# The memory branch: loads issued from ScalarE, norms moved behind the queries, two gate products pulled ahead

## The chip, the core and the metric

The kernel is written for one core of a Trainium2 chip. Such a core has TensorE (matrix products, PE in the rows, with PEld for its weight loads), VectorE (DVE), ScalarE (ACT), GpSimd (POOL) and SyncE (SP), which only issues transfers here. Each engine works through its own instructions in the order in which the program was built; semaphores hold an instruction until what it needs is there. The metric is the device time of one execution in microseconds.

## The reference

Two blocks of two layers each run on 512 tokens of width 1024 in float32. The first block (dilated attention, a recurrence, two feed-forward layers) ends at about 1550 us of the trace and is not touched. The second block repeats this layer twice:

```
h = rmsnorm(x, norm_g);  z = h @ w_in            # w_in: 1024 x 7968
o_a, o_b = two attention branches of parts of z
mem_kv = rmsnorm(mem, mem_norm_g) @ w_mem_kv     # mem: 256 rows of 1024
o_m = softmax(norm(q) @ norm(k).T / sqrt(128)) @ v, 4 heads of 128   # q of z; k, v of mem_kv
g = sigmoid(merge part of z), three gates of 1024
x = x + (g0 * (o_a @ w_branch_a) + g1 * (o_b @ w_branch_b) + g2 * (o_m @ w_branch_m)) @ w_out
```

The change is in the branch of `mem`, which comes first in each of the two layers.

## The kernel before

Every float32 product is made of three products of a high and a low part (`mm3`, L43 to L47). A weight unit of 512 KB is loaded by `wunit` (L212, a load that SyncE issues into one of two `ws` buffers), and split: ScalarE writes the high part `wh` (a CAST at L204), VectorE the low part `wl` (a subtraction at L204). There are four `wh` and four `wl` buffers, which come free when TensorE has read them. Of TensorE's eight output banks three are called `acc`, two `tr`, two `sc`, one `pv`.

The end of the layer before already computes the queries of the memory branch (`second_first`): one `acc` bank for each group of 128 tokens, groups 0 to 2 ahead of the branch, and group 3 when the branch asks for it. Each bank takes 24 products of 128x512, and the four weight units of the queries fill all four `wh` buffers until group 3 is through.

`memory` then copies each bank into two `zc` tiles (ScalarE, L1397; three buffers), and norms each: square (L813, ScalarE), sum and scaling (L815, L816, VectorE), a power (L817, GpSimd), two multiplications (L818, L1399, VectorE). It is turned by TensorE (L856, into a `tr` bank, two transposes for a tile) and split again (L204). The 256 rows of `mem` are loaded as two tiles, normed by `normed` (L309 ScalarE, L300 VectorE, L302 GpSimd, L312 VectorE), and turned by `turned` (L320, 16 transposes into `acc` and `sc` banks). Then come the products for keys and values (rows `acc<-wh,st`), which read the turned rows.

`weave` (L945 on) runs a branch step by step and, after the steps that a table PLANS names, one step of a filler. The filler is `branch`: gate products of 24 matmuls in two steps, and output products of 12 in one. A step is 12 matmuls whichever it is. What the branches leave of the filler runs on its own at the layer's end. A scheduler that simulates the program at build time sets the final order on each engine; `behind` keeps it from placing an instruction ahead of another that is named.

In a transfer or product, the rows name what is written, `<-`, and what is read; in a product the moving operand stands first.

Of the kernel before, what the change touches and what calls it, by code (L numbers as in the profile page):

```python
# [18 lines left out]
D = 1024  # L19
NT = T // 128  # L20
KD = D // 128
# [8 lines left out]
LRU_BUFS = 24  # L30
NORMALIZE_AFTER, VALUES_AFTER = 5, 6
LRU_STEPS = (0, 1, 2, range(4), "v", 3, range(4, 8), "vvv")
PLANS = ((16,),
         (8, 13, 13, 14, 15, 18, 19, 19, 22, 22, 25, 26, 26, 27, 27, 28, 28, 29, 29, 35, 35, 37, 38, 39),
         (1, 5, 5, 8, 8, 10, 12, 15, 16, 17, 19, 21, 32, 32, 34, 35, 38))
TURN_BANKS = (("acc", "sc"), ("acc", "sc"), ("sc", "tr"), ("tr", "pv"))
# [132 lines left out]
class Net:  # L169
# [618 lines left out]
    def state(self, shape, dt=F32R):  # L788
        return self.lt("st", shape, dt)

    def small_bc(self, row, n, name):
        t = self.lt(name, [128, n])
        self.nc.sync.dma_start(t, row[None, :].to_broadcast([128, n]))
        return t

    def rope_tables(self, g, scale=1.0):
# [160 lines left out]
    def second_layer(self, l, z2):  # L957
        nc, i, tc = self.nc, self.i, self.tc
        w_in, h = i["w_in_2"][l], self.h
        with tc.tile_pool(name=f"sec{l}", bufs=1) as self.lp:  # L960
            lp = self.lp
            u, o_m, o_a, o_b = [], [], [], []
            br = [self.branch(l, h, o, i[f"w_branch_{x}_2"][l], b, u) for o, x, b in ((o_m, "m", 2), (o_a, "a", 0), (o_b, "b", 1))]
            self.weave(self.memory(l, h, w_in, z2, o_m), br[0], PLANS[0])
            self.weave(self.nsa(l, h, w_in, o_a), itertools.chain(br[0], br[1]), PLANS[1])
            self.weave(br[0])
            self.weave(self.fox(l, h, w_in, o_b), itertools.chain(br[1], br[2]), PLANS[2])
# [40 lines left out]
    def branch(self, l, h, o, w, b, u):  # L1008
# [9 lines left out]
        def gate(m):  # L1018
            c = OFF_MG + b * D + m * 128
            wh, wl = self.wunit(wg[:, :, c:c + 128])  # L1020
            pg = self.bank()
            for k in range(KD):
                mm3(nc, pg, wh[:, k], wl[:, k], h[0][:, k], h[1][:, k], k == 0, k == KD - 1)
                if k == KD // 2 - 1:
                    yield
            t = self.lt("mt", [128, T])
            nc.scalar.activation(t, pg, AF.Tanh, scale=0.5)
            ts.append(t)
            yield
# [344 lines left out]
            nc.sync.dma_start(K[o:o + 2, e::2], self.cd[1, :, 4 * hf + e:4 * hf + 4:2])  # L1374


    def memory(self, l, h, w_in, z2, os):
        nc, i, lp = self.nc, self.i, self.lp
        lh, ll = self.rows(h)
        gq = self.small_bc(i["mem_q_norm_2"][l], 128, "gq")  # L1380
        gk = self.small_bc(i["mem_k_norm_2"][l], 128, "gk0")
        gm = self.lt("pt", [128, D])
        nc.sync.dma_start(gm, i["mem_norm_g_2"][l][None, :].to_broadcast([128, D]))
        mH, mL = self.state([128, KD, 256]), self.state([128, KD, 256])
        rows = []
        for t in range(2):
            mt, xn = self.lt("pt", [128, D]), self.lt("o", [128, D])
            nc.sync.dma_start(mt, i["mem_2"][0, t * 128:(t + 1) * 128])
            rows.append(self.normed(mt, gm, (xn[:, :512], xn[:, 512:], xn)))
        Q = [self.state([128, 2, 2, T]) for _ in range(2)]  # L1390
        for t, ps in enumerate(z2):
            if t >= 2:
                self.turned(rows[t - 2], (mH, mL), t - 2)
            cs = slice(t * 128, (t + 1) * 128)
            for c in range(2):
                zc = self.lt("zc", [128, 256])
                nc.scalar.copy(zc, ps[:, c * 256:c * 256 + 256])  # L1397
                qn = self.head_norm(zc, 2, 128)
                nc.vector.scalar_tensor_tensor(qn, qn, 128 ** -0.5, gq[:, None, :].to_broadcast([128, 2, 128]), op0=OP.mult, op1=OP.mult)  # L1399
                pt = self.transposed([qn[:, a] for a in range(2)])  # L1400
                self.split(Q[c][:, 0, :, cs], Q[c][:, 1, :, cs], pt[:, :256].rearrange("p (h q) -> p h q", h=2))
            yield
        wkv = i["w_mem_kv_2"][l]
        mlh, mll = self.rows((mH, mL))
        K = self.state([128, 2, 4, 256])
# [136 lines left out]
```

## Time and profile before

| | us |
|---|---|
| median of 3 runs | 2842.91 (2842.14 to 2843.55) |
| the profiled execution | 2847.33 |
| its span, first to last instruction | 2845.2 |
| TensorE busy | 2752.4 |
| VectorE busy | 1655.0 |
| ScalarE busy | 1285.5 |
| GpSimd busy | 509.2 |
| mean granted clock of TensorE | 0.988 |

TensorE is busy nearly throughout, so time is lost where it idles or where its granted clock is below 1. The memory branch begins at about 1550 us in layer 0 and at about 2205 us in layer 1, and the rows below are of these two places.

### The profile page before, as it was taken

Reading aid. Unit: us, or ns where it says so; the run is one execution under the profiler, and the core shown is the slowest. Engines: PE = TensorE matmul, PEld = TensorE weight load, DVE = VectorE, ACT = ScalarE, POOL = GpSimd, SP = SyncE. Lnnn points to the kernel's source line nnn. Section 1 sums busy time; section 2 is a strip of 40 time slices with the busy share of each in tenths; the row PEclk is TensorE's granted clock in tenths of the full one; section 3 lists DMA queues with packets and bytes.
Section 4 is the critical chain, followed back from the end, with each engine's and each line's share of the span. In section 5 each row is a group of like instructions: output and inputs, shape, how many; then the busy total and the mean of one; then the engine's idle time right before and its main releaser. Section 6 shows DMA issues by size and latency. Waiting matters only on the chain.

```text
span 2845.2 us, 39405 instructions
## 1 busy us (share of the span) xinstructions
PE 2752.4 (97%) x14493; PEld 2338.7 (82%) x14493; DVE 1655.0 (58%) x3306; ACT 1285.5 (45%) x2518; POOL 509.2 (18%) x682
## 2 busy tenths in 40 slices
PE   7999999799999998999998999999999899999999
PEld 6788888688888887888887898789878798788987
DVE  3245555555542678555425687776744677777753
ACT  3234344344432465444323554666533554665542
POOL 0001101111100000111001242333320242333420
PEclk9999999899999999999999999999999999999999
DMA  5553443333332343433323424122234423113233
GB/s 172 171 169 86 104 94 86 118 111 97 97 126 96 112 122 108 126 96 97 126 97 114 125 74 109 38 54 75 71 93 141 137 70 109 34 46 84 71 93 107
DMA packets 386071, 288.52 MB, mean 101 GB/s; under 512 B 33576, under 2 KB 339496, under 8 KB 385880
## 3 DMA queue, kind: packets, MB, share of 16 engines
q1 hardware_dynamic: 376752, 268.94, 32.9%
q10 hardware_dynamic: 9128, 17.07, 1.6%
q8 instruction: 115, 1.88, 0.3%
q14 instruction: 76, 0.62, 0.1%
HBM read 266.86 MB, written 21.20 MB: 101 GB/s over the span
## 4 chain that ended last, share of the span: by engine, by line
PE 82%; DVE 8%; DMA 4%; ACT 3%; issue 2%; POOL 1%; SPq 0%; ACTq 0%; DVEq 0%; POOLq 0%
PE acc L45 20%; PE acc L46 20%; PE acc L47 20%; PE tr L856 2%; PE sc L45 2%; PE sc L46 2%; PE sc L47 2%; DVE wl L204 2%; PE pv L916 2%; PE tr L45 2%; PE tr L47 1%; PE tr L46 1%; PE pv L46 1%; PE pv L47 1%; DMA ws<-in_attn_w_qkv_dram 1%
## 5 line engine op out<-in xcount | busy, mean ns | idle before, releaser
L204 DVE TENSOR_TENSOR wl<-ws,wh 128x1024 fp32r<-128x1024 f32 (+2 forms) x476 | 563.9, 1186 | 686.8 <-ACT wh L204 680.8
L204 ACT CAST wh<-ws 128x1024 fp32r<-128x1024 f32 (+2 forms) x476 | 469.5, 987 | 819.7 <-PE acc L46 303.6
L45 PE MATMUL acc<-hH,wh 128*128 128x512 f32 (+1 forms) x1928 | 742.3, 386 | 12.2 <-ACT gate L769 6.2
L46 PE MATMUL acc<-hL,wh 128*128 128x512 f32 (+1 forms) x1928 | 741.3, 385 | 1.5 <-DVE hL L204 1.2
L47 PE MATMUL acc<-hH,wl 128*128 128x512 f32 (+1 forms) x1928 | 739.5, 384 | 1.0 <-DVE wl L204 1.0
L45 PEld LDWEIGHTS acc<-hH,wh 128*128 128x128 f32 x1928 | 363.3, 189 | 83.6 <-ACT gate L769 6.6
L47 PEld LDWEIGHTS acc<-hH,wl 128*128 128x128 f32 x1928 | 363.9, 189 | 69.2 <-DVE wl L204 1.5
L46 PEld LDWEIGHTS acc<-hL,wh 128*128 128x128 f32 x1928 | 364.1, 189 | 68.4 <-DVE hL L204 2.5
L45 PE MATMUL acc<-wh,hH 128*128 128x256 f32 (+3 forms) x864 | 267.3, 312 | 5.4 <-ACT hH L204 4.1
L46 PE MATMUL acc<-wl,hH 128*128 128x256 f32 (+3 forms) x864 | 266.9, 310 | 2.3 <-DVE wl L204 2.3
L47 PE MATMUL acc<-wh,hL 128*128 128x256 f32 (+3 forms) x864 | 264.9, 309 | 0.1
L45 PEld LDWEIGHTS acc<-wh,hH 128*128 128x128 f32 x864 | 165.6, 192 | 14.5 <-ACT hH L204 4.5
L46 PEld LDWEIGHTS acc<-wl,hH 128*128 128x128 f32 x864 | 165.7, 192 | 11.9 <-DVE wl L204 3.7
L47 PEld LDWEIGHTS acc<-wh,hL 128*128 128x128 f32 x864 | 165.3, 191 | 7.4 <-DVE hL L204 0.4
L645 POOL TENSOR_TENSOR cv<-cv 128x512 f32<-128x512 f32 x48 | 62.0, 1292 | 465.1 <-DVE cv L582 448.4
L582 DVE SCALAR_TENSOR_TENSOR cv<-acc,cw,cv 128x511 f32<-128x511 f32 (+1 forms) x192 | 142.5, 746 | 3.2
L856 PE MATMUL tr<-ident,P 128*128 128x128 f32 x720 | 123.3, 277 | 10.7 <-DVE pt L204 5.2
L817 POOL TENSOR_TENSOR hst<-hst,mhalf 128x4 f32<-128x4 f32 (+2 forms) x90 | 91.0, 1017 | 223.5 <-DVE hst L816 221.7
L889 ACT ACTIVATE P<-P,soft 128x128 f32<-128x128 f32 (+1 forms) x192 | 108.1, 563 | 49.9 <-DVE soft L888 45.7
L888 DVE CUSTOM_DVE_ANT_0 P<-sc,causal 128x128 f32<-128x128 f32 (+1 forms) x192 | 92.9, 486 | 45.8 <-PE tr L856 31.5
L891 POOL TENSOR_SCALAR P<-P,soft,ngate 128x128 f32<-128x128 f32 (+3 forms) x128 | 83.9, 658 | 153.6 <-DVE soft L890 117.5
L204 DVE TENSOR_TENSOR pt<-tr,pt 128x128 fp32r<-128x128 f32 (+2 forms) x224 | 104.1, 474 | 11.8 <-ACT pt L204 10.4
(452 smaller groups left out, 4770.1 us busy)
## 6 DMA issues: line engine op xcount, KB each, us to landing
ws<-in_w_in_dram SPq DMA_DIRECT2D x116, 512.0 KB
ws<-in_ffn_w_up_dram SPq DMA_DIRECT2D x96, 512.0 KB
ws<-in_attn_w_qkv_dram SPq DMA_DIRECT2D x72, 512.0 KB
ws<-in_ffn_w_down_dram SPq DMA_DIRECT2D x48, 512.0 KB
x<-x ACTq DMA_DIRECT2D x16, 512.0 KB
ws<-in_lru_w_in_dram SPq DMA_DIRECT2D x16, 512.0 KB
ws<-in_w_mem_kv_dram SPq DMA_DIRECT2D x16, 512.0 KB
ws<-in_w_out_dram SPq DMA_DIRECT2D x16, 512.0 KB
```

The costliest lines, as they stand in the source:

```text
L45: nc.tensor.matmul(out, lh, rh, start=start, stop=False)
L46: nc.tensor.matmul(out, lh, rl, start=False, stop=False)
L47: return nc.tensor.matmul(out, ll, rh, start=False, stop=stop)
L204: return nc.scalar.copy(hi, src), (eng or nc.vector).tensor_tensor(lo, src, hi.bitcast(F32), op=OP.subtract)
L582: nc.vector.scalar_tensor_tensor(dst[:, s:], ps[:, :T - s], cw(taps - 1 - s), dst[:, s:], op0=OP.mult, op1=OP.add)
L645: nc.gpsimd.tensor_tensor(g, g, v, op=OP.mult)
L817: nc.gpsimd.tensor_tensor(st[:, 1], st[:, 0], self.mhalf[:rows, :nh], op=OP.pow)
L856: self.nc.tensor.transpose(ps[:, a * 128:(a + 1) * 128], s, self.ident)
L888: nc.vector.tensor_tensor_reduce(out=P, in0=S, in1=self.causal[:, 512 - n:512], scale=-1.0, scalar=BIG, op0=OP.add, op1=OP.min, accum_out=m)
L889: nc.scalar.activation(P, P, AF.Exp, bias=m, scale=-1.0, accum_out=s)
L891: nc.gpsimd.tensor_scalar(P, P, r, mult, op0=OP.mult, op1=OP.mult)
L916: nc.tensor.matmul(ps[:, lo:256], v(j), p[:, j, lo:], start=first and j == 0 and u == 0, stop=last and j == nj - 1 and u == 1)
```

## The change

Five loads (two gain vectors, the two tiles of `mem`, the gain of the memory norm) are issued by ScalarE instead of SyncE, the tiles ahead of their gain. `normed` of both tiles stands behind the last query tile's split, `turned` of both behind the second of two gate products. These two gates are the first four steps of the filler, which `memory` takes itself after the queries; the one step that the table took later is gone.

```diff
-PLANS = ((16,),
+PLANS = ((),
...
-    def small_bc(self, row, n, name):
+    def small_bc(self, row, n, name, eng=None):
         t = self.lt(name, [128, n])
-        self.nc.sync.dma_start(t, row[None, :].to_broadcast([128, n]))
+        (eng or self.nc.sync).dma_start(t, row[None, :].to_broadcast([128, n]))
...
-                mm3(nc, pg, wh[:, k], wl[:, k], h[0][:, k], h[1][:, k], k == 0, k == KD - 1)
+                self.last_gate = mm3(nc, pg, wh[:, k], wl[:, k], h[0][:, k], h[1][:, k], k == 0, k == KD - 1)
...
-        gq = self.small_bc(i["mem_q_norm_2"][l], 128, "gq")
-        gk = self.small_bc(i["mem_k_norm_2"][l], 128, "gk0")
+        gq = self.small_bc(i["mem_q_norm_2"][l], 128, "gq", nc.scalar)
+        gk = self.small_bc(i["mem_k_norm_2"][l], 128, "gk0", nc.scalar)
         gm = self.lt("pt", [128, D])
-        nc.sync.dma_start(gm, i["mem_norm_g_2"][l][None, :].to_broadcast([128, D]))
+        mts = [self.lt("pt", [128, D]) for _ in range(2)]
+        for t in range(2):
+            nc.scalar.dma_start(mts[t], i["mem_2"][0, t * 128:(t + 1) * 128])
+        nc.scalar.dma_start(gm, i["mem_norm_g_2"][l][None, :].to_broadcast([128, D]))
...
-        rows = []
-        for t in range(2):
-            mt, xn = self.lt("pt", [128, D]), self.lt("o", [128, D])
-            nc.sync.dma_start(mt, i["mem_2"][0, t * 128:(t + 1) * 128])
-            rows.append(self.normed(mt, gm, (xn[:, :512], xn[:, 512:], xn)))
...
-            if t >= 2:
-                self.turned(rows[t - 2], (mH, mL), t - 2)
...
-                self.split(Q[c][:, 0, :, cs], Q[c][:, 1, :, cs], pt[:, :256].rearrange("p (h q) -> p h q", h=2))
+                ends = self.split(Q[c][:, 0, :, cs], Q[c][:, 1, :, cs], pt[:, :256].rearrange("p (h q) -> p h q", h=2))
             yield
+
+        for n in range(4):
+            next(fill)
+        with behind(self.tc, *ends):
+            rows = []
+            for mt in mts:
+                xn = self.lt("o", [128, D])
+                rows.append(self.normed(mt, gm, (xn[:, :512], xn[:, 512:], xn)))
+        with behind(self.tc, self.last_gate):
+            for t in range(2):
+                self.turned(rows[t], (mH, mL), t)
```

TensorE before, in layer 0, right behind the queries of token group 2 (three query tiles, then four transposes of the first memory tile, then group 3 in bank 11562):

```order
L47 MATMUL acc_11493<-wh_11310,hL_10821 128x512
L856 MATMUL tr_11443<-ident_72,zc_11433 128x128 x2
L856 MATMUL tr_11458<-ident_72,zc_11448 128x128 x2
L856 MATMUL tr_11473<-ident_72,zc_11463 128x128 x2
L320 MATMUL acc_11518<-ident_72,o_11410 128x128 x4
L45 MATMUL acc_11562<-wh_11292,hH_10820 128x512
```

Three query tiles and a part of the first memory tile were turned ahead of group 3.

TensorE now, at the end of the second gate product (bank 11624); `zc_11570` is the eighth and last query tile, `o_11651` and `o_11660` are the two memory tiles, bank 11699 is the first of keys and values:

```order
L46 MATMUL acc_11624<-hL_10821,wh_11620 128x512
L856 MATMUL tr_11510<-ident_72,zc_11500 128x128 x2
L47 MATMUL acc_11624<-hH_10820,wl_11621 128x512
L856 MATMUL tr_11525<-ident_72,zc_11515 128x128 x2
L856 MATMUL tr_11565<-ident_72,zc_11555 128x128 x2
L856 MATMUL tr_11580<-ident_72,zc_11570 128x128 x2
L320 MATMUL acc_11669<-ident_72,o_11651 128x128 x4
L320 MATMUL sc_11676<-ident_72,o_11651 128x128 x4
L320 MATMUL acc_11683<-ident_72,o_11660 128x128 x4
L45 MATMUL acc_11699<-wh_11703,st_11411 128x512
```

Group 3 and both gates now stand ahead of most query transposes; the last three query tiles and all of the memory rows stand behind the second gate, and no product lies between them.

ScalarE before, in layer 0, from the first query copy on (`o_11410` and `o_11421` are the two memory tiles, `zc_11478` and `zc_11532` the fourth and fifth query tile):

```order
L1397 COPY zc_11433<-acc_11314 128x256
L1397 COPY zc_11448<-acc_11314 128x256
L1397 COPY zc_11463<-acc_11339 128x256
L813 ACTIVATE rt_11435<-zc_11433 128x256
L813 ACTIVATE rt_11450<-zc_11448 128x256
L813 ACTIVATE rt_11465<-zc_11463 128x256
L204 CAST st_11431<-tr_11443 128x2x128
L1397 COPY zc_11478<-acc_11339 128x256
L309 ACTIVATE o_11410,st_11412<-pt_11409 128x1024
L813 ACTIVATE rt_11480<-zc_11478 128x256
L204 CAST st_11432<-tr_11458 128x2x128
L1397 COPY zc_11532<-acc_11493 128x256
```

The fourth copy followed on the first split of a turned query tile and the fifth on the second, with one memory square between.

ScalarE now, from the last split of `h` to the first query copy:

```order
L204 CAST hH_10820<-pv_11385 128x4x128
L793 DMA gq_11401<-in_mem_q_norm_2_dram 128x128
L793 DMA gk0_11403<-in_mem_k_norm_2_dram 128x128
L1385 DMA pt_11406<-in_mem_2_dram 128x1024
L1385 DMA pt_11407<-in_mem_2_dram 128x1024
L1386 DMA pt_11405<-in_mem_norm_g_2_dram 128x1024
L1393 COPY zc_11415<-acc_11314 128x256
```

The five issues stand between the split, whose end lets the last products of the queries run, and the copy that begins to free the first bank.

ScalarE now, from the first three query squares on; 11585 and 11618 are the gates' weights, 11701 and 11721 the first two units of keys and values, `zc_11460` and `zc_11500` the fourth and fifth query tile:

```order
L813 ACTIVATE rt_11447<-zc_11445 128x256
L204 CAST wh_11587<-ws_11585 128x1024
L204 CAST wh_11620<-ws_11618 128x1024
L204 CAST wh_11703<-ws_11701 128x1024
L204 CAST st_11413<-tr_11425 128x2x128
L1393 COPY zc_11460<-acc_11339 128x256
L204 CAST st_11414<-tr_11440 128x2x128
L1393 COPY zc_11500<-acc_11475 128x256
L813 ACTIVATE rt_11462<-zc_11460 128x256
L813 ACTIVATE rt_11502<-zc_11500 128x256
L204 CAST wh_11721<-ws_11719 128x1024
L204 CAST wh_11739<-ws_11737 128x1024
```

Splits of weights now stand between the query tiles' squares and the copies of the next tiles; before, the fourth query copy followed directly on the first split of a turned tile.

ScalarE now, around the eighth query copy; 11743 is the fourth unit of keys and values, whose `wh` buffer was that of the second gate:

```order
L204 CAST wh_11745<-ws_11743 128x1024
L204 CAST st_11413<-tr_11510 128x2x128
L1393 COPY zc_11570<-acc_11530 128x256
L1027 ACTIVATE mt_11649<-acc_11624 128x512
L204 CAST st_11414<-tr_11525 128x2x128
L813 ACTIVATE rt_11572<-zc_11570 128x256
L204 CAST st_11413<-tr_11565 128x2x128
L204 CAST st_11414<-tr_11580 128x2x128
L309 ACTIVATE o_11651,st_11652<-pt_11406 128x1024
L309 ACTIVATE o_11660,st_11661<-pt_11407 128x1024
```

The memory norms, which stood between the query tiles before, now stand behind the last of them, and the eighth copy stands behind the split of a weight unit.

## Rows read from the trace of the kernel before

**Rows 1.** the page, first line and part 1.

```profile
span 2845.2 us, 39405 instructions
...
PE 2752.4 (97%) x14493; PEld 2338.7 (82%) x14493; DVE 1655.0 (58%) x3306; ACT 1285.5 (45%) x2518; POOL 509.2 (18%) x682
```

**Rows 2.** busy time by stretch, layer 0 and layer 1: stretch, then length and engines.

```profile
1549.90:1570.00 20.10, 12.21 (x50) 9.35 (x49) 14.71 (x39) 9.74 (x24) 5.69 (x8) 0.66 0.35 116
...
2205.60:2223.10 17.50, 11.03 (x51) 8.66 (x50) 13.92 (x36) 8.49 (x18) 5.69 (x8) 0.80 0.40 128
```

**Rows 3.** TensorE in time, layer 0: start, length, engine, line, operation, wait before it.

```profile
1549.64 0.39 PE L47 MATMUL acc<-wh,hL 128*128 128x512 f32 x1
1553.01 0.66 PE L856 MATMUL tr<-ident,zc 128*128 128x128 f32 x2 [2.98 <-DMA gk<-in_mem_k_norm_dram]
...
1559.85 1.08 PE L320 MATMUL acc<-ident,o 128*128 128x128 f32 x4 [4.28 <-ACT o L309]
...
1561.15 0.63 PE L46 MATMUL acc<-wl,hH 128*128 128x512 f32 x1
1561.58 0.63 PE L47 MATMUL acc<-wh,hL 128*128 128x512 f32 x1
...
1565.78 0.40 PE L45 MATMUL acc<-wh,hH 128*128 128x512 f32 x1
1566.01 0.39 PE L46 MATMUL acc<-wl,hH 128*128 128x512 f32 x1
...
1569.63 0.60 PE L320 MATMUL sc<-ident,o 128*128 128x128 f32 x4
1569.99 0.47 PE L45 MATMUL acc<-wh,st 128*128 128x512 f32 x1
```

**Rows 4.** what TensorE waited for, layer 0, 1531 to 1570: total, times, longest.

```profile
PE acc L320 <- ACT o L309: 4.3, 1, 4.3
PE tr L856 <- DMA gk<-in_mem_k_norm_dram: 3.0, 1, 3.0
```

**Rows 5.** ScalarE in time, layer 0.

```profile
1548.51 0.59 ACT L204 CAST hH<-pv 128x512 fp32r<-128x512 f32 x1
1548.98 0.94 ACT L1397 COPY zc<-acc 128x256 f32<-128x256 f32 x3
...
1553.70 0.37 ACT L204 CAST st<-tr 128x256 fp32r<-128x256 f32 x1 [2.57 <-PE tr L856]
...
1556.80 1.06 ACT L309 ACTIVATE o<-pt 128x1024 f32<-128x1024 f32 x1 [2.45 <-DMA pt<-in_mem_dram]
...
1579.33 1.05 ACT L204 CAST wh<-ws 128x1024 fp32r<-128x1024 f32 x1 [1.55 <-DMA ws<-in_w_mem_kv_dram]
```

**Rows 6.** SyncE's queue in time, layer 0.

```profile
1548.56 0.34 SPq L793 DMA_DIRECT2D gq<-in_mem_q_norm_dram  x1
...
1549.89 0.91 SPq L1388 DMA_DIRECT2D pt<-in_mem_dram  x2
1550.85 1.61 SPq L793 DMA_DIRECT2D gk<-in_nsa_k_norm_dram  x2
...
1575.22 0.37 SPq L212 DMA_DIRECT2D ws<-in_w_mem_kv_dram  x1
```

**Rows 7.** VectorE in time, layer 0.

```profile
1558.95 1.41 DVE L312 SCALAR_TENSOR_TENSOR o<-pt,st 128x512 f32<-128x512 f32 x2
...
1571.51 1.22 DVE L204 TENSOR_TENSOR wl<-ws,wh 128x1024 fp32r<-128x1024 f32 x1 [0.26 <-ACT wh L204]
```

**Rows 8.** TensorE and ScalarE in time, layer 1.

```profile
2205.41 0.39 PE L47 MATMUL acc<-wh,hL 128*128 128x512 f32 x1
...
2203.84 0.94 ACT L1397 COPY zc<-acc 128x256 f32<-128x256 f32 x3
```

**Rows 9.** busy time by stretch, later stages of layer 0.

```profile
1700.00:1800.00 100.00, 95.51 (x600) 80.76 (x598) 75.77 (x221) 54.90 (x134) 30.78 (x48) 1.00 0.34 94
...
2000.00:2100.00 100.00, 95.63 (x509) 81.02 (x509) 64.97 (x143) 49.55 (x114) 33.07 (x39) 0.98 0.29 77
```

More of the change, by code (lines that the diff above doesn't have):

```diff
@@ L963, in second_layer @@
             br = [self.branch(l, h, o, i[f"w_branch_{x}_2"][l], b, u) for o, x, b in ((o_m, "m", 2), (o_a, "a", 0), (o_b, "b", 1))]
-            self.weave(self.memory(l, h, w_in, z2, o_m), br[0], PLANS[0])
+            self.weave(self.memory(l, h, w_in, z2, o_m, br[0]), br[0], PLANS[0])
             self.weave(self.nsa(l, h, w_in, o_a), itertools.chain(br[0], br[1]), PLANS[1])
@@ L1374, in decay_keys, with memory @@
             nc.sync.dma_start(K[o:o + 2, e::2], self.cd[1, :, 4 * hf + e:4 * hf + 4:2])
-    def memory(self, l, h, w_in, z2, os):
+    def memory(self, l, h, w_in, z2, os, fill):
         nc, i, lp = self.nc, self.i, self.lp
         lh, ll = self.rows(h)
-        gq = self.small_bc(i["mem_q_norm_2"][l], 128, "gq")
-        gk = self.small_bc(i["mem_k_norm_2"][l], 128, "gk0")
+        gq = self.small_bc(i["mem_q_norm_2"][l], 128, "gq", nc.scalar)
+        gk = self.small_bc(i["mem_k_norm_2"][l], 128, "gk0", nc.scalar)
         gm = self.lt("pt", [128, D])
-        nc.sync.dma_start(gm, i["mem_norm_g_2"][l][None, :].to_broadcast([128, D]))
+        mts = [self.lt("pt", [128, D]) for _ in range(2)]
+        for t in range(2):
+            nc.scalar.dma_start(mts[t], i["mem_2"][0, t * 128:(t + 1) * 128])
+        nc.scalar.dma_start(gm, i["mem_norm_g_2"][l][None, :].to_broadcast([128, D]))
         mH, mL = self.state([128, KD, 256]), self.state([128, KD, 256])
-        rows = []
-        for t in range(2):
-            mt, xn = self.lt("pt", [128, D]), self.lt("o", [128, D])
-            nc.sync.dma_start(mt, i["mem_2"][0, t * 128:(t + 1) * 128])
-            rows.append(self.normed(mt, gm, (xn[:, :512], xn[:, 512:], xn)))
         Q = [self.state([128, 2, 2, T]) for _ in range(2)]
         for t, ps in enumerate(z2):
-            if t >= 2:
-                self.turned(rows[t - 2], (mH, mL), t - 2)
             cs = slice(t * 128, (t + 1) * 128)
```

## The prediction

> **What bounds the kernel now.** The page's first line and table of engines come first: TensorE is busy 2752.4 of 2845.2 us [rows 1]. A change can therefore win or lose only where TensorE idles or runs slowly, so the next view is its busy time by stretch. Later stages run at 95.5 and 95.6 of 100 us with a granted clock of 1.00 and 0.98 [rows 9]. The two starts of the memory branch are the exception: 12.21 of 20.10 us in layer 0 with a clock of 0.66, and 11.03 of 17.50 us in layer 1 with 0.80 [rows 2].
>
> How much is lost there? At the clock's upper level (2.4 GHz) matmuls follow each other by 0.23 us (1565.78 to 1566.01), four transposes take 0.36 us (1569.63 to 1569.99), so 0.09 each; at the lower level (1.2 GHz), behind the long wait, matmuls follow by 0.43 us (1561.15 to 1561.58) [rows 3]. Layer 0's stretch holds 50 records [rows 2]: 24 matmuls of query group 3 and 26 transposes, so 5.5 + 2.3 = 7.8 us of work; 20.1 − 7.8 = 12.3 us lost, of which 20.1 − 12.2 = 7.9 are idle and 4.4 slow clock. Layer 1's holds 51 records, 7.9 us of work; 9.6 lost, 6.5 idle and 3.1 slow. **21.9 us is lost in both, all that the change could win here.**
>
> The view of waits puts 3.0 us of layer 0 on the load of `gk`, ahead of the first query transposes, and 4.3 us on the memory row's norm (ScalarE, L309), ahead of its first turn [rows 4]. ScalarE in time shows why the norm was late: its square at 1556.80 waited 2.45 us for the row's load [rows 5].
>
> **The change part by part.** Gates only move. A step of the filler is 12 matmuls whichever it is, so four steps taken here are missing as cover later, where one was missing before (step 16). That later cover has the same kind of steps and TensorE is 95% busy there [rows 9], so I cost it at nothing, with ±3 us for the sum. What decides is whether TensorE's loss at the start shrinks. I walk layer 0 through the new order with durations of before. Groups and gates are 24 × 0.23 = 5.5 us.
>
> *(a) Five issues on ScalarE.* SyncE took from 1548.56 to 1550.85 for these loads [rows 6], 2.29 us, and nothing waited behind it. On ScalarE the first query copy waits behind them: 1548.98 becomes 1551.27. Two copies of 0.31 (0.94 for three) [rows 5] free the bank that group 3 needs: about 1552.0. TensorE ends group 2 at 1549.64 + 0.39 = 1550.03 [rows 3], so it idles 2.0. In layer 1 group 2 ends at 2205.80 and the copy would stand at 2203.84 + 2.29 = 2206.13 [rows 8], two copies done at 2206.8: 1.0. Bounds: 0, if issues run beside other work, to 2.3. I take the sum, since SyncE's issues are the nearest rows. The loads gain little from it: on SyncE both tiles were issued by 1550.80 [rows 6], and on ScalarE, from 1549 on, they are issued about as late.
>
> The Trainium skill, "DMA: Bandwidth & Descriptors", section "Issuing engines are not separate DMA queues", says that transfers end on the same 16 DMA engines whoever issues them, and that another issuer saves only sequencer time, "usually small relative to the DMA itself". By that remark (a) would be near 0 and the forecast 3 us lower; the 2.29 us of [rows 6] are against calling it small here.
>
> *(b) Weight splits ahead of the query copies.* Group 3 runs 1552.0 to 1557.5, four transposes to 1557.9. Gate 0 takes the bank of group 1, which needs `zc_11460` copied. In ScalarE's order that copy stands behind the split of `wh_11703`, the first unit of keys and values, and this one needs a `ws` buffer that gate 0's unit holds until VectorE's `wl`. Gate 0's `wh` buffer is free after six matmuls of group 3 (1553.4); its split takes 1.05 [rows 5], `wl` 1.22 [rows 7], so 1555.7 at the earliest; I add 0.8 for the query sums ahead of it on VectorE. Then the load: a single one issued at 1575.22 [rows 6] let its split start at 1579.33 [rows 5], 4.1 us. So 1560.6; split 1.05, tile split 0.37, copy 0.31 [rows 5]: 1562.3. Idle 4.4. Bounds: 0.8 if the load is not the last to come, 6.4 if the 1.5 MB of rows delay it by 2.
>
> *(c) Gate 1's bank.* Gate 0 ends at 1567.8, four transposes to 1568.2. The copy that frees the next bank stands behind the split of the third unit, which needs gate 0's `wh`: 1567.8 + 1.05 + 0.37 + 0.31, 1569.6 with the hand-overs. Idle 1.4.
>
> *(d) The tail behind gate 1.* It ends at 1575.1. The fourth unit's split, which needs gate 1's `wh`, stands ahead of the eighth query copy: 1.05 + 0.37, copy at 1576.5. From a copy to its turn it took 1548.98 to 1553.01 [rows 3, 5], 4.0 us with some wait for `gk` in it, but the `wl` of the unit now stands in VectorE's way, so I keep 4.0: 1580.5. Turn 0.3, split 0.37: 1581.2. Only now may ScalarE begin the row's square; from there to the row's first turn took 1556.80 to 1559.85 [rows 3, 5], 3.05 us, with VectorE's two multiplications of 1.41 in it [rows 7]: 1584.3. The second row follows by its square and read, 1.3: 1585.6. Its transposes and their split take 1.3 more, and the first product of keys starts at **1586.9**. These 11.8 us hold 24 transposes, 2.2 us; idle 9.6. No product is left to cover it: both gates stand ahead. All that waits behind it on TensorE is the whole of keys and values.
>
> Two waits are thus gone (3.0 and 4.3) [rows 4], and the ends that come last in their place are the splits of weights in (b) and (c) and the norm chain in (d).
>
> Sum, layer 0: 2.0 + 4.4 + 1.4 + 9.6 = 17.4 idle; layer 1 with 1.0 for (a): 16.4. The slow clock behind the two long gaps I take as the mean of before, 3.8 a layer. Lost after: 17.4 + 16.4 + 7.6 = 41.4, against 21.9: **+19.5 us**. The profiled execution took 2847.3, 2.1 beyond its span; with the change 2866.8. It lies 4.4 above the median of 2842.9, so the median to expect is **2862**.
>
> The Trainium skill, "TensorE: Matmul & The Clock Gate", section "HAM oscillation — how this bites in real kernels", warns that waits between bursts of matmuls bring the lower clock back at each burst. By that rule all four gaps of a layer, not only the long two, could be followed by slow matmuls; the trace agrees so far as the slow spacing of 0.43 us stands behind the 4.28 us wait [rows 3]. The sum would be up to 4 us higher, which the range holds.
>
> **Rivals.**
>
> *The gates cover the waits (faster).* Two gates give 11 us of products per layer where TensorE waited 7.3 for loads and norms [rows 4], and the rows' loads land early enough. If nothing stood between gate 1 and the keys, all 21.9 would go: 2842.9 − 21.9 = 2821; half of it would give 2832. The order speaks against it: the norms may not start before the last query tile's split, which is itself behind gate 1, so the cover ends before what it should cover begins. It decides if the key products start within 3 us of gate 1's end. 10%.
>
> *Only the tail remains (same).* The loads of units come early and issues cost nothing, so (a) to (c) vanish: idle 2 × 9.6 = 19.2, plus 4 to 7.6 for the clock, against 21.9: +1 to +5, 2844 to 2848. For it: the split at 1579.33 waited only 1.55 us for its load [rows 5]. Against it: the `ws` buffer of the first unit is free only after gate 0's `wl`. 13%.
>
> *The loads starve (slower still).* The unit loads share the DMA engines with the rows and come 2 us later, in both (b) and (c): 2 × 4 = 8 us more, 2870. The DMA share in the stretch was only 0.35 [rows 2], which speaks against it. 7%.
>
> *It doesn't do what it says.* The rows' loads come no earlier from ScalarE's queue, but no step above needs them earlier: the norms now start at 1581, long after 1556.8. This changes no number and belongs to the forecast.
>
> **How the numbers follow.** The forecast has 70%. Low end: no issue cost, (b) at 0.8, no slow clock: 2 × (0.8 + 1.4 + 9.6) = 23.6 against 21.9, +1.7, 2845. High end: 41.4 + 1.2 (clock at 4.4 a layer) + 4 (two loads 2 us late) + 3 (later cover) = 49.6, +27.7, 2871. The faster rival lies below it, what is beyond 2871 is a part of the starving one; so the range is 2845 to 2871. A measurement of this kernel tells 0.2% (5.7 us) from no change: faster is below 2837.2, slower above 2848.6. Faster 10%; same 13%, the tail alone; slower 77%.
>
> **What would show it.** In the profile of the changed kernel: (a) the first query copy some 2.3 us later than the last split of `h`, and a gap of 2 ahead of group 3; (b) a gap of about 4 ahead of gate 0, with ScalarE's split of the first unit waiting for its load; (c) a gap of 1.4 ahead of gate 1; (d) some 10 us with nothing but transposes between gate 1 and the first product of keys, which starts at about 1587 instead of 1570 (with 11 us of gates moved ahead, which are then missing later). The forecast is wrong if that last stretch is short, if the copies do not wait for splits of weights, or if the later cover has grown short or long by more than 3 us.

## The result and the profile after

The changed kernel takes 2882.5 us (median of 4 runs, 2876.6 to 2884.6), the kernel before 2843.2 (4 runs): a ratio of 1.0134, 95% interval 1.0117 to 1.0152. It is 39 us slower; the forecast was 2862, 19 us slower, with a range to 2871. The direction was right, the size half of what came.

The page of the changed kernel, first line and part 1:

```profile
span 2882.8 us, 39415 instructions
...
PE 2761.6 (96%) x14493; PEld 2345.8 (81%) x14493; DVE 1654.9 (57%) x3306; ACT 1287.3 (45%) x2518; POOL 522.7 (18%) x682
```

TensorE is busy 9 us longer than before [rows 1], and the span is 37.6 us longer. To see where, both traces are cut at four marks: the end of the queries of group 2 and the first product of keys (`acc<-wh,st`), in each layer. Before, these stand at 1550.0, 1570.0, 2205.8 and 2223.1. Busy time by stretch for the two long stretches of before (the columns of [rows 2]; its short ones are there):

```profile
1570.00:2205.80 635.80, 621.23 (x3714) 541.51 (x3711) 424.74 (x1029) 334.19 (x781) 187.40 (x258) 1.00 0.31 86
2223.10:2845.20 622.10, 605.55 (x3608) 528.48 (x3606) 409.23 (x1002) 318.25 (x755) 187.67 (x253) 0.99 0.29 82
```

and for all four of the changed kernel:

```profile
1551.00:1590.80 39.80, 25.63 (x101) 19.84 (x101) 23.41 (x53) 17.67 (x38) 7.76 (x10) 0.80 0.37 124
1590.80:2224.00 633.20, 613.23 (x3661) 535.53 (x3659) 415.59 (x1011) 326.22 (x762) 192.97 (x256) 0.99 0.30 83
2224.00:2262.50 38.50, 24.76 (x100) 19.37 (x101) 23.29 (x53) 17.67 (x38) 7.75 (x10) 0.80 0.39 127
2262.50:2882.80 620.30, 594.15 (x3557) 518.70 (x3555) 400.03 (x987) 311.80 (x740) 191.43 (x251) 0.99 0.28 78
```

Two gates, 11.0 us of products, now run in each short stretch and are missing in the long one behind it. With that taken into account, the starts lost 39.8 − 20.0 − 11.0 = 8.9 us (with the marks to a hundredth) and 38.5 − 17.3 − 11.0 = 10.2 us more than before; the long stretches 633.2 − 635.8 + 11.0 = **8.4** and 620.3 − 622.0 + 11.0 = **9.2** us. The untouched part ahead of the first mark adds 1.0. So the starts cost 19.1 us, as much as the forecast's whole sum of 19.5, and as much again is lost where the forecast had put 0 ± 3.

The start itself, TensorE in time, layer 0 (answers to [rows 3]):

```profile
1550.63 0.39 PE L47 MATMUL acc<-wh,hL 128*128 128x512 f32 x1
1553.65 0.50 PE L45 MATMUL acc<-wh,hH 128*128 128x512 f32 x1 [2.63 <-ACT zc L1393]
...
1564.31 0.63 PE L45 MATMUL acc<-hH,wh 128*128 128x512 f32 x1 [2.88 <-ACT zc L1393]
1564.73 0.63 PE L46 MATMUL acc<-hL,wh 128*128 128x512 f32 x1
...
1573.11 0.50 PE L45 MATMUL acc<-hH,wh 128*128 128x512 f32 x1 [1.01 <-ACT zc L1393]
1573.45 0.40 PE L46 MATMUL acc<-hL,wh 128*128 128x512 f32 x1
1573.68 0.39 PE L47 MATMUL acc<-hH,wl 128*128 128x512 f32 x1
...
1578.60 0.48 PE L47 MATMUL acc<-hH,wl 128*128 128x512 f32 x1
...
1581.45 0.55 PE L856 MATMUL tr<-ident,zc 128*128 128x128 f32 x2 [2.15 <-DVE st L204]
1584.07 0.66 PE L856 MATMUL tr<-ident,zc 128*128 128x128 f32 x2 [2.07 <-DVE zc L1395]
1587.94 1.09 PE L320 MATMUL acc<-ident,o 128*128 128x128 f32 x4 [3.21 <-DVE o L312]
...
1590.84 0.78 PE L45 MATMUL acc<-wh,st 128*128 128x512 f32 x1
```

All four gaps of the forecast are there: 2.63 us ahead of group 3, 2.88 ahead of gate 0, 1.01 ahead of gate 1, and behind gate 1 (1578.60) nothing but transposes for 12.2 us, up to the first product of keys at 1590.84. ScalarE shows what stood in the way (answers to [rows 5, 6]):

```profile
1549.69 0.34 ACTq L793 DMA_DIRECT2D gq<-in_mem_q_norm_dram  x1
1550.06 0.46 ACTq L793 DMA_DIRECT2D gk<-in_mem_k_norm_dram  x1
1550.55 0.93 ACTq L1385 DMA_DIRECT2D pt<-in_mem_dram  x2
1551.52 1.39 ACTq L1386 DMA_DIRECT2D pt<-in_mem_norm_g_dram  x1
1552.95 0.92 ACT L1393 COPY zc<-acc 128x256 f32<-128x256 f32 x3 [2.86 <-DMA gq<-in_mem_q_norm_dram]
...
1562.67 1.04 ACT L204 CAST wh<-ws 128x1024 fp32r<-128x1024 f32 x1 [3.32 <-DMA ws<-in_w_mem_kv_dram]
...
1578.66 1.05 ACT L204 CAST wh<-ws 128x1024 fp32r<-128x1024 f32 x1 [3.95 <-PE acc L46]
...
1579.88 0.38 ACT L1393 COPY zc<-acc 128x256 f32<-128x256 f32 x1
...
1585.04 1.06 ACT L309 ACTIVATE o<-pt 128x1024 f32<-128x1024 f32 x1
```

The five issues fill 1549.69 to 1552.91, and the first query copy comes behind them. The idle time of 2.86 us is put down to a landing, but what came last was the issue at 1551.52. The split at 1562.67 is that of the first unit of keys, 3.32 us late for its load, with the copy for gate 0 behind it. The split at 1578.66 stands ahead of the eighth copy at 1579.88, and the row's square begins only at 1585.04.

In the long stretch no single wait stands out. TensorE's waits there, before (total us, times, longest):

```profile
PE acc L45 <- ACT o L204: 2.3, 1, 2.3
...
PE sc L1160 <- DVE soft L888: 1.2, 3, 0.4
```

and in the changed kernel:

```profile
PE acc L45 <- ACT o L204: 3.4, 2, 2.3
...
PE sc L1160 <- DVE soft L888: 2.2, 4, 0.7
...
PE acc L46 <- DVE wl L204: 1.0, 1, 1.0
...
PE acc L45 <- DVE sl L933: 0.9, 1, 0.9
```

TensorE's idle time in this stretch went from 14.6 to 20.0 us (length less busy time above), and the granted clock from 1.00 to 0.99, by several waits of about a microsecond: an output product now waits for the second branch's own `sl` (L933, at 1786.40, in its attention), another for `o`, a split comes late (`wl`), and the scores of the second branch's attention wait 2.2 instead of 1.2 us for its maxima (`soft`).

### The profile page after: what moved, and what is told of

The parts are those of the page before. It is cut to its first block, busy times and chain, and to the rows that moved or that the text cites. A ratio compares the mean times of both kernels' runs of the same rounds, so it can differ in the third digit from the quotient of the medians.

```text
span 2882.8 us, 39415 instructions
## 1 busy us (share of the span) xinstructions
PE 2761.6 (96%) x14493; PEld 2345.8 (81%) x14493; DVE 1654.9 (57%) x3306; ACT 1287.3 (45%) x2518; POOL 522.7 (18%) x682
## 5 line engine op out<-in xcount | busy, mean ns | idle before, releaser
L204 DVE TENSOR_TENSOR wl<-ws,wh 128x1024 fp32r<-128x1024 f32 (+4 forms) x476 | 568.2, 1195 | 705.4 <-ACT wh L204 700.7
L204 ACT CAST wh<-ws 128x1024 fp32r<-128x1024 f32 (+4 forms) x476 | 469.7, 987 | 836.1 <-PE acc L46 321.9
L45 PE MATMUL acc<-wh,hH 128*128 128x256 f32 (+3 forms) x864 | 267.8, 312 | 12.3 <-ACT hH L204 4.1
```

Of the source, the lines that this page charges most:

```text
L45: nc.tensor.matmul(out, lh, rh, start=start, stop=False)
L204: return nc.scalar.copy(hi, src), (eng or nc.vector).tensor_tensor(lo, src, hi.bitcast(F32), op=OP.subtract)
```

## The experiments

The table gives for each kernel the change against before of the four stretches, cut at the same marks (where group 3 follows group 2 without a gap, the mark is put 24 × 0.23 us ahead of its end) and with 5.5 us moved for each gate that runs in the short one, read from one profile each; then the median against that of before on the same chip, in us. The first block, which no kernel touches, ended up to 5.7 us earlier in these profiles than in that of before, so stretches and medians are compared, not spans. A microsecond or two in a stretch is nothing. The four stretches of each kernel add up to 2 to 9 us less than the change of its median: the profiled execution of before took 4.4 us more than its median, and some of the others took less than theirs (changed, cut first: 4.5 us). The stretches tell where time is lost, the medians how much.

| kernel | start, layer 0 | rest, layer 0 | start, layer 1 | rest, layer 1 | median | ratio, 95% interval |
|---|---|---|---|---|---|---|
| changed | +8.9 | +8.4 | +10.2 | +9.2 | +39.3 | 1.0117 to 1.0152 |
| no gates | +10.8 | −1.9 | +10.7 | −4.3 | +17.8 | 1.0047 to 1.0077 |
| gates alone | +0.3 | +9.0 | +0.5 | +6.4 | +17.9 | 1.0047 to 1.0077 |
| sync loads | +3.8 | +8.4 | +3.5 | +8.0 | +27.0 | 1.0078 to 1.0108 |
| four at 16 | 0.0 | +6.6 | 0.0 | +6.5 | +15.3 | 1.0036 to 1.0069 |
| cut three | −0.5 | +2.8 | +0.1 | +2.4 | +9.3 | 1.0020 to 1.0049 |
| two at 16 | −0.1 | +10.7 | −0.4 | +6.5 | +24.7 | 1.0073 to 1.0103 |
| scalar loads | +0.6 | +5.1 | +0.6 | +3.7 | +13.8 | 1.0036 to 1.0066 |
| free norms | −5.4 | +11.4 | −3.0 | +9.4 | +16.9 | 1.0038 to 1.0071 |
| cut first | −0.1 | +2.9 | +0.3 | −0.6 | +7.9 | 1.0016 to 1.0036 |
| free, cut first | −4.2 | +5.9 | −2.7 | +3.0 | +9.4 | 1.0023 to 1.0049 |
| last gate | −3.6 | +1.0 | −2.6 | −3.9 | −6.2 | 0.9967 to 0.9985 |
| changed, cut first | +7.3 | +8.4 | +3.9 | +7.1 | +35.4 | 1.0106 to 1.0136 |
| last gate, summed | −3.6 | +0.1 | −2.8 | −3.4 | −7.8 | 0.9965 to 0.9985 |
| three and 16 | −5.6 | +8.4 | −3.7 | +3.4 | +4.6 | 1.0008 to 1.0026 |
| rows first | −2.3 | +1.9 | −0.2 | −0.6 | +0.9 | 0.9995 to 1.0013 |
| changed, last gate | +8.0 | −1.9 | +10.3 | +0.1 | +18.9 | 1.0056 to 1.0083 |

**No gates.** The changed kernel without the four steps:

```diff
-PLANS = ((),
+PLANS = ((16,),
...
-        for n in range(4):
-            next(fill)
...
-        with behind(self.tc, self.last_gate):
+        with behind(self.tc, *ends):
             for t in range(2):
                 self.turned(rows[t], (mH, mL), t)
```

> The changed kernel without the four filler steps behind the queries (step 16 has its one step back; the memory rows are turned behind the last query split). The start of the branch lost 19.0 us more than before in the changed kernel, everything behind it 17.6 us more. Theory A, the four early steps shift the filler and cost the later branches the 17.6: the later part is back at the time of before, and the start costs the rows' chain without gates, about 1 to 3 us a layer, so 2845 to 2850. Theory B, the 17.6 come from the norms and loads, which make the planner order everything else anew: the later part keeps its 17.6, so 2860 to 2868.

Measured 2858.6. The rest is back at (or under) the time of before, as theory A says; theory B is out, though its total nearly fits: the start alone, without gates, costs 10.8 and 10.7 us, where 1 to 3 had been expected.

**Gates alone.** Only the four steps, in the kernel before:

```diff
-PLANS = ((16,),
+PLANS = ((),
...
             yield
+        for n in range(4):
+            next(fill)
         wkv = i["w_mem_kv_2"][l]
```

> The kernel before with the four filler steps behind the queries and nothing else (loads on SyncE, norms and turns where they were). Theory A (the shifted filler costs 17.6 later): the start gains at most a few us, as products now stand behind the rows' chain, and the later part loses 17.6: 2855 to 2862. Theory B (norms and loads): the later part as before, 2838 to 2845.

Measured 2858.7. Theory A: 15.4 us in the rest. The start gains nothing: the planner puts the gates behind the rows' turns, so both waits of [rows 4] stay (2.98 and 4.24 us).

**Sync loads.** The changed kernel with all five loads as here:

```diff
-            nc.scalar.dma_start(mts[t], i["mem_2"][0, t * 128:(t + 1) * 128])
+            nc.sync.dma_start(mts[t], i["mem_2"][0, t * 128:(t + 1) * 128])
```

> The changed kernel with the five loads back on SyncE. If the issues on ScalarE hold the first query copies as forecast (2.3 us; the gap ahead of group 3 was 2.63 us in layer 0 and 0.69 in layer 1), 3 us less than the changed kernel: 2879. If issues cost nothing because the load of gq ends last anyway: 2882.5, and the gap ahead of group 3 stays.

Measured 2867.7: a miss for both. By the medians against before it takes 12.3 us less than the changed kernel, where 3 or nothing had been expected. The starts lose 5.1 and 6.7 us less. Not the gap ahead of group 3 alone went (2.63 us to none), but also most of that ahead of gate 0 (2.88 to 0.74 us), since the planner now lays the fourth query copy ahead of the first split of keys.

**Four at 16**, in the kernel before:

```diff
-PLANS = ((16,),
+PLANS = ((16, 16, 16, 16),
```

> The kernel before with four filler steps at step 16 of the memory branch instead of one, so that the start is as before and the later branches get the filler of the changed kernel. Theory A (the shift of the filler costs 17.6 later): 2856 to 2861, with the start as before. Theory B (norms, loads, or the lack of any step at 16 cost it): 2841 to 2846.

Measured 2856.0: theory A. Busy time by stretch:

```profile
1546.30:1566.20 19.90, 11.35 (x48) 9.00 (x49) 14.67 (x38) 9.55 (x23) 5.68 (x8) 0.74 0.35 117
1566.20:2208.60 642.40, 624.00 (x3714) 543.09 (x3712) 424.15 (x1029) 335.04 (x781) 194.58 (x258) 0.99 0.31 86
2208.60:2226.00 17.40, 10.93 (x52) 8.75 (x51) 13.73 (x36) 8.29 (x18) 5.69 (x8) 0.80 0.41 126
2226.00:2854.50 628.50, 606.63 (x3607) 527.62 (x3605) 407.14 (x1002) 319.95 (x755) 192.15 (x253) 0.99 0.29 81
```

The starts are those of before to 0.1 us, and the long stretches, with all their work in them, take 6.6 and 6.5 us more than 635.8 and 622.0. Three more steps pulled ahead are thus enough for 13.1 of the 17.6 us; the norms, loads and pins are not needed for these.

**Two at 16**, in the kernel before, and **cut three**, in the kernel with four at 16:

```diff
-PLANS = ((16,),
+PLANS = ((16, 16),
```

```diff
-          ... 29, 29, 35, 35, 37, 38, 39),
+          ... 29, 29, 35, 35),
```

> The kernel before with two filler steps at step 16 of the memory branch instead of one; nothing else. Theory T1 (cost by the number of steps taken early): a third of the 15.3 us of four steps, so 2845 to 2847. Theory T2 (cost by alignment): a shift by one puts output products where gates stood, all through both tables, and costs as much as or more than the shift by three: 2855 or more.

> The kernel with four steps at 16, and the last three entries of the second branch's table dropped, so that the third branch and the pure tail get the very filler steps of the kernel before. With four at 16 the second branch lost 1.5 to 3 us a layer more than before, the third branch about 5 a layer, 15.3 in all. Theory T1 (each step taken early leaves a later stretch without cover): the loss moves to the end of the second branch, three steps of 2.7 us a layer, and the total stays near 2856. Theory T2 (it is the alignment: which product, with which input, stands at a table's step): the third branch is back at the time of before, and what is left is the second branch's, 2844 to 2850.

Two at 16 measured 2864.4, 24.7 us slower: one step pulled ahead costs more than three. Theory T1, a price by the number of steps, is out. With three entries cut 2849.1: three steps are missing in the second branch, and yet the kernel loses 9.3 us instead of 15.3 (medians against before), as expected by T2; the third branch again runs the steps that it ran before.

**Scalar loads.** The five loads alone (the tiles ahead of their gain), in the kernel before, with its norms and turns where they were:

```diff
-            nc.sync.dma_start(mt, i["mem_2"][0, t * 128:(t + 1) * 128])
+            nc.scalar.dma_start(mts[t], i["mem_2"][0, t * 128:(t + 1) * 128])
```

> The kernel before with the five loads issued by ScalarE (tiles ahead of their gain) and nothing else. By step (a) of the forecast the first query copies come 2.3 us later, and the first turn of a query tile, which waited 3.0 us for gk, comes up to 2.3 later: 0 to 2 us a layer, 2841 to 2846. Rival: the issue costs the 5 to 7 us a layer by which the changed kernel and the same with loads on SyncE differ at the start: 2851 to 2854.

Measured 2853.5: the rival's sum, but in another place. The starts lost 0.6 us each, as step (a) had it; 5.1 and 3.7 us came right behind them, among the products of keys and values. ScalarE in time:

```profile
1546.65 0.92 ACT L1399 COPY zc<-acc 128x256 f32<-128x256 f32 x3 [2.88 <-DMA gk<-in_nsa_k_norm_dram]
...
1551.37 1.06 ACT L309 ACTIVATE o<-pt 128x1024 f32<-128x1024 f32 x1 [3.17 <-DMA pt<-in_mem_dram]
```

The first copy again waits 2.88 us behind the issues, and the row's square 3.17 us for its load, against 2.45 before [rows 5]: the loads came no earlier from this queue.

**Free norms.** The changed kernel with loads on SyncE, and the norms written ahead of the queries without a pin:

```diff
-        with behind(self.tc, *ends):
-            rows = []
-            for mt in mts:
-                ...
+        rows = []
+        for mt in mts:
+            ...
         Q = [self.state([128, 2, 2, T]) for _ in range(2)]
```

> The changed kernel with loads on SyncE and the memory rows' norms not held behind the last query split (the planner may place them between the query tiles, as before); the turns stay behind the second gate. If the place of the norms is what keeps 9.6 us a layer idle behind the gates (step (d)): the gates now cover the rows' chain, the start loses some 5 us a layer less than before, the later part about 17 more: 2845 to 2850. Rival, the query tiles' own chain (copy, norm, turn behind the second gate) keeps TensorE idle whatever the rows do: 2860 to 2866.

Measured 2856.6, some 7 us above the expected range and below the rival's. Its start says that the place of the norms is what kept step (d) idle: 9.2 and 6.5 us less lost than with the norms pinned (sync loads), 5.4 and 3.0 less than before. The rest lost 20.8, more than the 17 expected.

**Cut first**, in the kernel with four at 16, in the one with free norms, and in the changed kernel, so that from the fourth entry on both tables run the steps of before:

```diff
-          (8, 13, 13, 14, 15, 18, ...
+          (14, 15, 18, ...
```

> The kernel with four steps at 16, and the first three entries (8, 13, 13) of the second branch's table dropped. From its fourth entry on every table entry now runs the very filler step of the kernel before, in both later branches, and the tail is as long. T2 (alignment is what costs): the 13.5 us of the kernel with four at 16 shrink to what the missing cover at steps 8 and 13 costs, 0 to 4 us in all, so 2840 to 2845. T1 (steps taken early are missing as cover): three steps of 2.7 us a layer stand bare, 2850 or more.

> The changed kernel with loads on SyncE, norms placed by the planner, turns behind the second gate, and the first three entries of the second branch's table dropped. The start lost 8.3 us less than before in the kernel without the dropped entries, and its later part 21 more. If alignment is the cause, the later part is back within 4 us: 2832 to 2838, faster than before by 0.1 to 0.3%. If not, 2848 or more.

> The changed kernel with nothing but the first three entries of the second branch's table dropped. If alignment is the cause of the 17.6 to 18.1 us behind the start: these go but for 0 to 4, the start keeps its 19, so 2863 to 2868 (if the other chip's 3 us stand in between, 2860 to 2868). If it is not: 2878 or more.

Measured 2848.3, 2849.7 and 2875.8, and none is where alignment alone would put it. The first lies between its two ranges: 2.3 of 13.1 us are left in the rest, but 7.9 of 15.3 by the median. The second lies in the range that was written down for the case that alignment is not the cause, the third between its two ranges and nearer to that one: 8.9 and 15.5 us stay in the rest, and 9.4 of 16.9 and 35.4 of 39.3 by the medians. By the medians, tables that run the steps of before from the fourth entry on give back half of the loss at most.

With the work that TensorE had done lined up (each product counted by its shortest usual spacing), the changed kernel's rest of layer 0 lost some 5.6 us between 1656 and 1781 us of before (second branch) and 4.8 between 1845 and 1936 (into the third). Of the 4.8, at most 0.9 us are left in the last two kernels; but between 1752 and 1781 they lose about 6 us, where the first, with the same entries cut, loses nothing. That is a loss of the second branch alone. It lies where that branch's attention begins. Busy time in the 14 us from its first score (`sc<-st`, L1160) in layer 0, before, in the changed kernel, in the first of the three here and in the third:

```profile
1765.92:1779.92 14.00, 12.52 (x62) 9.66 (x62) 12.21 (x46) 7.81 (x23) 6.62 (x10) 1.00 0.40 110
...
1779.87:1793.87 14.00, 10.73 (x49) 7.67 (x49) 11.10 (x49) 7.99 (x24) 5.73 (x10) 0.98 0.33 88
...
1765.91:1779.91 14.00, 12.51 (x62) 9.58 (x61) 12.70 (x48) 8.01 (x24) 6.60 (x11) 1.00 0.40 113
...
1780.34:1794.34 14.00, 9.05 (x32) 5.87 (x31) 10.43 (x50) 8.34 (x28) 6.64 (x11) 0.67 0.20 57
```

Of TensorE's 62 instructions before, 33 are products into `acc` banks, which stand among the scores; in the changed kernel there are 23, in the first of the three 32. In the second and third the last such product ends as the scores begin, so nothing covers the attention's waits, and TensorE idles 5.4 and 5.0 us instead of 1.5 (14.00 less busy time), at a granted clock of 0.76 and 0.67.

**Three and 16.** The kernel with free norms and the first entries cut:

```diff
-PLANS = ((),
+PLANS = ((16,),
...
-        for n in range(4):
+        for n in range(3):
```

> The kernel with free norms and three entries dropped, with three of its four early steps taken behind the queries and the fourth at step 16 of the memory branch. If the missing step at 16 is what kept 8.9 us in its second branch: the later part loses 2 to 3 us as in the kernel with four at 16 and three entries dropped, the start gains about 7: 2834 to 2840. If the dropped entries or the start cost it: 2846 to 2850.

Measured 2845.7, just under the second range. It does not tell the two apart: the planner ran the fourth step ahead of the keys too (48 gate products there, as before), so the step at 16 was in the table only. Its attention in the second branch, too, begins with no product beside it (8.57 of 14 us busy).

**The gate from the far end.** The kernel with free norms, and one gate from the filler of the third branch, whose steps run in the pure tail:

```diff
-PLANS = ((),
+PLANS = ((16,),
...
-            self.weave(self.memory(l, h, w_in, z2, o_m, br[0]), br[0], PLANS[0])
+            self.weave(self.memory(l, h, w_in, z2, o_m, br[2]), br[0], PLANS[0])
...
-            t = self.lt("mt", [128, T])
+            t = self.lt("me" if b == 1 and m == 0 else "mt", [128, T])
...
-        for n in range(4):
+        for n in range(2):
             next(fill)
```

> As the kernel with free norms, but only one gate product is taken early, and it is taken from the third branch's filler (whose steps run in the pure tail, with a tile of its own for the result), so that both tables run the steps of the kernel before, step 16 included. If alignment is the cause: the later part as before, and the start between that with two gates (8.3 us less) and before: 2833 to 2839. If early steps cost because the planner lays everything behind them anew: 2850 or more.

Measured 2834.2; this kernel starts the sum of the branches anew with the third, so the products of the first two are lost, and the next adds them (`first = not u` becomes `first = b == 2`):

> The kernel with one gate taken from the third branch's filler, now with the third branch's products added to those of the other two (in the kernel last_gate they started the sum anew, and so the first two were lost). That is eight additions a layer on GpSimd, beside TensorE's work in the tail. Theory T2 (alignment): as last_gate, 2832 to 2838, faster than before by 0.1 to 0.3%. Rival: the additions at the tail's end stand on the path, 2840 or more.

Measured 2833.3, 9 runs against 25 of before: a ratio of 0.9975, 0.9965 to 0.9985. It is the fastest kernel here. Busy time by stretch:

```profile
1544.90:1566.80 21.90, 16.05 (x75) 12.63 (x74) 18.11 (x39) 14.79 (x32) 5.69 (x7) 0.92 0.56 185
1566.80:2197.20 630.40, 618.11 (x3686) 539.46 (x3687) 421.71 (x1027) 328.68 (x771) 188.79 (x259) 0.99 0.30 84
2197.20:2217.20 20.00, 15.88 (x75) 12.58 (x73) 15.99 (x37) 12.32 (x25) 5.69 (x7) 0.91 0.59 189
2217.20:2830.40 613.20, 596.68 (x3581) 521.22 (x3581) 405.70 (x1002) 314.77 (x750) 186.52 (x254) 0.99 0.29 81
```

and TensorE in time at its start:

```profile
1549.94 0.40 PE L47 MATMUL acc<-wh,hL 128*128 128x512 f32 x1
...
1551.55 0.44 PE L856 MATMUL tr<-ident,zc 128*128 128x128 f32 x2 [0.99 <-DVE zc L1399]
1553.54 0.79 PE L45 MATMUL acc<-hH,wh 128*128 128x512 f32 x1 [1.55 <-ACT zc L1397]
...
1565.17 0.41 PE L856 MATMUL tr<-ident,zc 128*128 128x128 f32 x2 [2.10 <-DVE zc L1399]
1566.78 0.58 PE L45 MATMUL acc<-wh,st 128*128 128x512 f32 x1 [1.20 <-ACT zc L1397]
```

Group 3 follows group 2 without a gap, the loads and norms run beside it and the gate, and of the waits of 3.0 and 4.3 us [rows 4] four of 1.0 to 2.1 us are left (the first end at 1549.94 is that of group 3).

**Rows first.** The kernel before, with only the order of three loads changed:

```diff
+        for t in range(2):
+            nc.sync.dma_start(mts[t], i["mem_2"][0, t * 128:(t + 1) * 128])
         nc.sync.dma_start(gm, i["mem_norm_g_2"][l][None, :].to_broadcast([128, D]))
...
-            nc.sync.dma_start(mt, i["mem_2"][0, t * 128:(t + 1) * 128])
```

> The kernel before with the two tiles of mem loaded ahead of their gain (on SyncE) and nothing else. If the order of the loads gives the 6 us that the start gains in the kernels with free norms: 2833 to 2836, and the 4.3 us wait for the row's norm is down to 2 or less. If that gain needs a gate between norm and turn: 2839 to 2842.

Measured 2842.1, no change (0.9995 to 1.0013). The start of layer 0 gains 2.3 us, that of layer 1 0.2: the wait for the row's norm is down to 0.20 us, but one of 3.36 us for a query tile stands in its place. The order of the loads alone does not give the gain.

**Changed, last gate.** The changed kernel with the diff of the gate from the far end (and the same line on `first`): one gate, from the third branch's filler:

> The changed kernel (loads on ScalarE, norms behind the last query split, turns behind the gate) with one gate only, taken from the third branch's filler, so that both tables run the steps of before, step 16 included. If the shift of the filler is the whole cause of the 18 us behind the start: the later part as before within 3, the start 19 to 22 more, 2858 to 2864. If the changed start itself disturbs the second branch: 2868 to 2876.

Measured 2860.0. Busy time by stretch:

```profile
1546.00:1579.50 33.50, 20.27 (x78) 15.30 (x77) 21.92 (x52) 16.50 (x36) 6.88 (x10) 0.73 0.39 132
1579.50:2207.90 628.40, 616.34 (x3685) 539.00 (x3683) 418.10 (x1012) 327.16 (x764) 186.29 (x256) 0.99 0.30 84
2207.90:2241.00 33.10, 19.71 (x76) 14.96 (x77) 21.52 (x52) 16.52 (x36) 8.21 (x10) 0.74 0.40 131
2241.00:2857.70 616.70, 598.67 (x3581) 523.06 (x3579) 402.33 (x988) 312.41 (x742) 181.70 (x251) 0.99 0.28 80
```

The starts lose what they lose in the changed kernel (8.0 and 10.3 us, one gate taken off), and the rest is that of before (−1.9 and +0.1). **With loads, norms and pins as changed, and the filler's steps not shifted, nothing is lost behind the start.** The kernel also takes one gate early instead of two and runs the step at 16; no run takes two gates from the far end.

## Why the prediction was wrong

**Right: the start, step by step.** (a) 2.0 and 1.0 us forecast ahead of group 3, 2.63 and 0.69 measured; (b) 4.4, 2.88 in layer 0 and 4.26 in layer 1; (c) 1.4, 1.01 in both; (d) the stretch from gate 1's end to the first product of keys 11.8, some 11.8 measured (1579.08 to 1590.84). That the sum came within half a microsecond (19.1 against 19.5) is partly luck, since the split between idle time and slow clock was off in opposite ways: TensorE idles 39.8 − 25.6 = 14.2 us in layer 0 where 17.4 stood, but the 101 records there are 73 products (one at the stretch's edge) and 28 transposes, some 19.1 us of work, so 6.5 us went to the lower clock where 3.8 stood. The transposes of (d) ran at it too (1.09 us for four at 1587.94, 0.60 before at 1569.63). A small misreading: the 50 records of layer 0 before [rows 2] hold 24 transposes, not 26, which is 0.2 us.

**Wrong: "That later cover has the same kind of steps ..., so I cost it at nothing, with ±3 us for the sum."** It cost 17.6 us, and so the prediction's own last sign of being wrong came. What failed is the step from "the same kind of steps" to "the same time". The tables name steps of the branches, and the filler has its own order: gate, gate, then an output product, which needs what the branch before has just made. Three steps pulled ahead move each entry of both tables on to another product. As the order repeats after three steps, it is one of the same kind in 36 of the 41 entries. In the other five it is not: at the first entry of either table the second half of a gate becomes an output product, and near the second branch's end one gate becomes an output product and two outputs become gates of the next filler.

Four at 16 shows the price alone (13.1 us in the stretches), two at 16 that it does not go by number (one step 16.7, three 13.1), and the changed start with unshifted tables that nothing of the rest is left without the shift (−1.8 instead of +17.6). Part of it can be seen where the second branch's attention begins: among its first 14 us of layer 0, 33 products into `acc` banks stand before and TensorE idles 1.5 us; in the changed kernel and in the one with four at 16 there are 23, and it idles 3.3, which is 1.8 of the 8.4 us; with the table cut and early gates none, and it idles 5.0 to 5.4; in the changed kernel with the last gate 52, and it does not idle. Two at 16 has 52 there too, so its loss lies elsewhere. Busy time of 95 of 100 us [rows 9] was read as cover to spare; it was measured with the steps where they stood.

Not settled is why the planner leaves this attention bare when the first three entries are cut in the kernels with early gates, and not in the one with four steps at 16, nor how much of the 17.6 us belongs to single entries. No run separates that.

**The rivals.** "The gates cover the waits" named a real gain that this order could not give: with norms left free, and the gate from the far end, the start gains 3.6 and 2.8 us. "It decides if the key products start within 3 us of gate 1's end": they started 11.8 later. The tail alone and the starved loads had too small a sum, as they too held the rest at nothing.

**The rules weighed.** The Trainium skill, "DMA: Bandwidth & Descriptors", section "Issuing engines are not separate DMA queues", calls the issue time usually small relative to the DMA itself. That is not the comparison that counted here: the five issues were paid out of ScalarE's own work, its first query copy waited 2.86 us behind them in layer 0, and the loads alone, on ScalarE, made the kernel 13.8 us slower.

By "TensorE: Matmul & The Clock Gate" of the Trainium skill, section "HAM oscillation — how this bites in real kernels", waits between bursts bring the lower clock back. The trace agrees for some gaps and not for others: behind the gap of 2.88 us products follow each other by 0.42 us (1564.31 to 1564.73), behind that of 1.01 us by 0.23 (1573.45 to 1573.68). The granted clock of the changed start is 0.80 with more slow time (6.5 us against some 4.5), and in the kernel with the faster start it is 0.92.

## What to carry to other kernels

A filler that is woven in by a table of positions is tuned to its phase: taking a step early shifts every later entry, and the price appears up to hundreds of microseconds behind the edit, in many waits of a microsecond or two. Take early cover from the end of the work that nothing is tuned to (here the pure tail), and the rest stays as it was. And work that is to hide a chain must not be what the chain waits for: with one and the same gate the start lost 8 to 10 us where the norms were held behind the queries (and the loads issued by ScalarE), and gained about 3 where both were free.

## What was not expected of the hardware

The same five loads took 2.29 us to issue on SyncE [rows 6] and 3.2 us on ScalarE in layer 0 (1549.69 to 1552.91). But the difference is one issue, that of the memory norm's gain, with 1.39 us; in layer 1 the same issue on ScalarE took 0.44 us:

```profile
2223.51 0.44 ACTq L1386 DMA_DIRECT2D pt<-in_mem_norm_g_dram  x1
```

All five took 2.28 us there (2221.67 to 2223.95), as on SyncE. So these runs do not show that ScalarE issues more slowly; what made the one issue long is open. What they show is that on ScalarE the issues stop the engine's own work: in both layers the first query copy started 0.04 us behind the last of them, and in layer 0 of sync loads, without them, right behind the split of `h`.
